# Attention on one core: sixteen softmax groups on VectorE with three passes each, in place of fourteen with three to four, and a new written-out order

## The chip, the cores and the metric

The kernel runs on one core of a Trainium2 chip. The metric is the device time of one execution in microseconds (us), here the median of three runs. The core's engines work side by side, each on its own instruction stream in order: TensorE (PE) multiplies matrices into PSUM, VectorE (DVE) and ScalarE (ACT) read PSUM and SBUF, GpSimd (POOL) works on SBUF here, and SyncE (SP) issues the DMAs.

## The reference

```python
# q, k, v: 8 batches x 8 heads x 512 positions x 64, float32
scale = 1.0 / np.sqrt(q.shape[-1])
scores = np.einsum('bhqd,bhkd->bhqk', q, k) * scale
attn = np.exp(scores - scores.max(axis=-1, keepdims=True))
attn = attn / attn.sum(axis=-1, keepdims=True)
out = np.einsum('bhqk,bhkd->bhqd', attn, v)
```

## The kernel before, in words

The 64 heads are taken as 32 pairs. For each pair, q and k are loaded in float32 (one 256 KB DMA each), cast to float16 by GpSimd, and turned so that the 64 features lie on partitions: 22 pairs, the first among them, by PE (steps `T`, followed by a VectorE copy `C` into the tile `tqk`), ten by a transposing DMA (steps `u`).

A **group** is 128 keys of both heads of a pair (for the first and last pair: two blocks of one head) against all 512 queries. Its scores fill one buffer `st` of 128x1024 float32 in PSUM (step `S`, L289: two matmuls that run side by side on the two halves of PE's rows). There are three such buffers; the number after the dot in `S57.0` is the buffer. The groups number 0 to 128; 127 and 128 are two halves of the last one. Most groups are exponentiated by ScalarE in one instruction (L295), which writes the float16 tile `pt`.

Fourteen groups (`KIND`) are exponentiated by VectorE instead, by building the float16's bits with a polynomial. For most of them PE first adds a constant to the scores (`lift`, L275, two more matmuls), so that the low 16 bits of a float32 score are the fraction of the exponent. Step `r` (L317) copies the scores from PSUM to a float32 tile `z`; steps `p` (L350, L331) are passes of `scalar_tensor_tensor` over 128x1024 elements. Kinds C and F take `r` and three passes, all on VectorE; S and X take `r` and two, with two GpSimd instructions (step `m`, L365 and L368) between them. The last pass of C, F and S reads `y` and `z`, both in SBUF, and writes 32-bit words to a tile `pd`. The buffer `st` of such a group is free again after the last pass that reads it.

Step `V` (L420) multiplies 128 queries of `pt` with v and a column of ones, four matmuls of 65 columns over the four blocks of keys; seven such results share one PSUM bank `o`. `R` and `N` (L385, L393) take the reciprocal of the ones' column and scale into the SBUF tile `ring`, and `O` stores 1 or 2 heads. `B` steps are matmuls on constants whose result is not used. `L` and `F` are V, R, N and the store for the last half head.

All of this is issued in the order of the string `ORDER`, written out by hand as one list of steps; each engine's instructions stand in the order in which the list names them, and waits between engines follow from the tiles. A cast step `cq4+p5.0` also waits for the VectorE step named behind the plus sign; 31 casts have such a wait. Pools set the rest: seven raw tiles for each of q, k and v (`RAW`), six of `qkp`, seven of `tqk`, 30 of `pt` and 4 of `pd`.

Of the kernel before, what the change touches and what calls it, by code (L numbers as in the profile page):

```python
# [37 lines left out]
T9.0.0 lk17 cq12 V4.0.3.39.1 T9.1.0 S34.2 cv6 lq16 V4.1.0.40.1 C9 V4.1.1.41.1 cq13 S35.0 lv13 R35.7
p30.1 T10.0.0 T10.1.0 lq17 S36.2 lk18 C10 S37.1 cv5+p30.1 S38.0 N35.7 ck12 T11.0.0 lv12 T11.1.0
p30.2 S39.2 V4.1.2.42.1 V4.1.3.43.1 V5.0.0.44.1 S40.1 C11 cv7+p30.1 ck13 r39 S41.0 lv14 T12.0.0 cv8  # L40
lq18 T12.1.0 S42.1 lk19 cv10 C12 V5.0.1.45.1 lq19 V5.0.2.46.1 ck14 V5.0.3.47.1 p39.0 V5.1.0.48.1
O21.1 S43.0 V5.1.1.49.0 O35.1 V5.1.2.50.0 V5.1.3.51.0 V6.0.0.52.0 lv15 S44.1 R42.7 ck15 p39.1
V6.0.1.53.0 lk20 ck16 S45.0 cq14+r39 lk21 V6.0.2.54.0 N42.7 S46.2 V6.0.3.55.0 p39.2 lv17 T13.0.1
T13.1.1 S47.1 lk22 R49.7 S48.0 C13 cv9+R49.7 O42.1 S49.2 r47 cv12 V6.1.0.56.1 V6.1.1.57.1
V6.1.2.58.1 cq15 V6.1.3.59.1 S50.0 N49.7 lv16 V7.0.0.60.1 ck17 V7.0.1.61.1 V7.0.2.62.1 p47.0 S51.2
lq20 V7.0.3.63.0 cv11 V7.1.0.64.0 V7.1.1.65.0 lq21 V7.1.2.66.0 S52.0 cq16 R56.7 N56.7 V7.1.3.67.0
lq22 V8.0.0.68.0 ck18+N49.7 p47.1 S53.2 lq23 V8.0.1.69.0 T14.0.1 cq17 T14.1.1 lk23 S54.0 R63.7 C14
S55.1 cq18+R63.7 lv19 N63.7 S56.2 T15.0.1 O49.1 p47.2 T15.1.1 V8.0.2.70.0 V8.0.3.71.0 lk24
V8.1.0.72.0 S57.0 C15 lq24 S58.1 V8.1.1.73.0 r57 V8.1.2.74.0 ck19+C15 T16.0.1 lk25 T16.1.1 S59.2
cq19 lv18 V8.1.3.75.0 C16 V9.0.0.76.0 cq20 S60.1 O56.1 R70.7 ck20 V9.0.1.77.1 N70.7 lq25 S61.2 p57.0  # L50
V9.0.2.78.1 V9.0.3.79.1 O63.1 T17.0.0 cq21+p47.2 T17.1.0 S62.1 cv13+C1 lk26 C17 S63.0 V9.1.0.80.1
V9.1.1.81.1 p57.1 lk27 V9.1.2.82.1 S64.2 V9.1.3.83.1 lq26 V10.0.0.84.0 V10.0.1.85.0 V10.0.2.86.0
R77.7 cv15+C17 V10.0.3.87.0 V10.1.0.88.0 N77.7 V10.1.1.89.0 lq27 V10.1.2.90.0 ck21+p57.0 S65.0 R84.7
S66.1 N84.7 T18.0.1 lk28 S67.2 p57.2 lv20 V10.1.3.91.0 T18.1.1 V11.0.0.92.0 lv22 S68.0 C18
ck22+p57.2 lq28 r68 S69.1 cq22+C18 T19.0.1 lk29 V11.0.1.93.0 cq23 V11.0.2.94.0 S70.2 O70.1 p68.0
ck23 V11.0.3.95.0 T19.1.1 V11.1.0.96.0 cq24 V11.1.1.97.0 S71.1 R91.7 S72.0 m68.0 N91.7 S73.2 u22 C19
S74.1 r72 T20.0.1 V11.1.2.98.0 T20.1.1 u23 V11.1.3.99.0 S75.2 C20 V12.0.0.100.0 V12.0.1.101.0 p72.0
S76.1 lk30 cv14 V12.0.2.102.0 V12.0.3.103.0 V12.1.0.104.0 V12.1.1.105.1 ck24 S77.2 lv21 R98.7 p72.1
V12.1.2.106.1 lq29 ck25 S78.1 u24 V12.1.3.107.1 N98.7 cq25 V13.0.0.108.1 V13.0.1.109.1 S79.0 p68.2
V13.0.2.110.1 T21.0.0 u25 T21.1.0 V13.0.3.111.1 S80.1 C21 ck26 S81.2 S82.0 cq26+r5 R105.7 lq30 r81  # L60
V13.1.0.112.0 V13.1.1.113.0 O77.1 V13.1.2.114.0 cq27 V13.1.3.115.0 V14.0.0.116.0 S83.1 lq31 cv16
V14.0.1.117.0 N105.7 V14.0.2.118.0 cq28 lv23 S84.0 p81.0 V14.0.3.119.1 cv17 lk31 V14.1.0.120.1
V14.1.1.121.1 V14.1.2.122.1 S85.1 cv19 R112.7 V14.1.3.123.1 N112.7 V15.0.0.124.1 ck27 V15.0.1.125.1
S86.0 lv24 R119.7 p81.1 V15.0.2.126.0 lv26 V15.0.3.127.0 V15.1.0.128.0 ck28 V15.1.1.129.0
V15.1.2.130.0 S87.1 cv18 N119.7 V15.1.3.131.0 V16.0.0.132.0 S88.2 cv21+R119.7 lv25 R126.7
V16.0.1.133.1 N126.7 V16.0.2.134.1 cq29 O91.1 V16.0.3.135.1 V16.1.0.136.1 V16.1.1.137.1 S89.0 u26
p72.2 V16.1.2.138.1 V16.1.3.139.1 V17.0.0.140.0 V17.0.1.141.0 S90.2 V17.0.2.142.0 R133.7 ck29 O98.1
V17.0.3.143.0 N133.7 V17.1.0.144.0 S91.1 u27 p81.2 V17.1.1.145.0 S92.0 S93.2 V17.1.2.146.0
V17.1.3.147.1 r93 V18.0.0.148.1 cv20+p81.2 lv28 V18.0.1.149.1 V18.0.2.150.1 S94.1 O105.1 cq30
V18.0.3.151.1 V18.1.0.152.1 R140.7 V18.1.1.153.1 ck30 u28 N140.7 S95.0 S96.2 cv22 R147.7  # L70
V18.1.2.154.0 N147.7 V18.1.3.155.0 cv23 V19.0.0.156.0 V19.0.1.157.0 O112.1 V19.0.2.158.0
V19.0.3.159.0 p93.0 lv27 S97.0 V19.1.0.160.0 V19.1.1.161.1 V19.1.2.162.1 V19.1.3.163.1 R154.7
cv25+C2 V20.0.0.164.1 S98.2 N154.7 S99.1 m93.0 u29 S100.0 r99 V20.0.1.165.1 V20.0.2.166.1
V20.0.3.167.1 V20.1.0.168.0 V20.1.1.169.0 lv29 S101.2 V20.1.2.170.0 R161.7 O119.1 V20.1.3.171.0
N161.7 V21.0.0.172.0 V21.0.1.173.0 S102.0 u30 p99.0 V21.0.2.174.0 V21.0.3.175.1 V21.1.0.176.1
V21.1.1.177.1 V21.1.2.178.1 cv24+r99 S103.2 R168.7 V21.1.3.179.1 O126.1 cv26+R161.7 N168.7
V22.0.0.180.1 V22.0.1.181.1 S104.1 O133.1 R175.7 m99.0 S105.0 N175.7 V22.0.2.182.0 O147.1
V22.0.3.183.0 V22.1.0.184.0 O154.1 V22.1.1.185.0 V22.1.2.186.0 p93.2 V22.1.3.187.0 S106.2 O161.1
V25.0.0.188.0 O161.0 S107.1 V25.0.1.189.1 R182.7 V25.0.2.190.1 lv30 N182.7 S108.0 V25.0.3.191.1 r108
V25.1.0.192.1 V25.1.1.193.1 V25.1.2.194.1 S109.2 V25.1.3.195.1 V23.0.0.196.0 V23.0.1.197.0 R189.7  # L80
V23.0.2.198.0 S110.0 N189.7 cq31 S111.1 p99.2 S112.2 V23.0.3.199.0 V23.1.0.200.0 V23.1.1.201.0
V23.1.2.202.0 V23.1.3.203.1 V26.0.0.204.1 ck31+r5 R196.7 S113.0 r111 V26.0.1.205.1 cv27+C2 u31
S114.2 cv28 V26.0.2.206.1 N196.7 V26.0.3.207.1 V24.0.0.208.1 V24.0.1.209.1 S115.0 O168.0 R203.7
V24.0.2.210.0 p108.0 V24.0.3.211.0 O175.1 V24.1.0.212.0 S116.2 O182.1 V24.1.1.213.0 V24.1.2.214.0
N203.7 lv31 V24.1.3.215.0 m108.0 S117.0 p111.0 O189.1 V26.1.0.216.0 V26.1.1.217.1 O203.1
# [15 lines left out]
def kernel(  # L101
# [29 lines left out]
    for m, kind in KIND.items():  # L131
        (g, c, _), (g2, c2, _) = groups[m]
        assert 0 < g == g2 < LAST and c == c2
        if kind in LIFTED:
            raises.setdefault(g, set()).add(c)
# [126 lines left out]
    def scores(m, b):  # L262
# [34 lines left out]
        )  # L297

# [331 lines left out]
```

## Time and profile before

| | before |
|---|---|
| three runs | 116.27, 116.42, 116.73 us; median 116.42 |
| the profiled execution | 116.05 us, of which span 114.3 us |
| ScalarE busy | 107.0 us, 94% of the span, 119 instructions |
| TensorE busy | 103.8 us, 91%, 1549 matmuls |
| VectorE busy | 103.5 us, 91%, 178 instructions |
| GpSimd busy | 76.5 us, 67%, 110 instructions |
| granted TensorE clock | full in each of the 40 slices |

The busy time of an engine is the time in which at least one of its instructions was under way. Instructions of one engine overlap at their ends, so the mean duration of one is longer than the distance from its start to the start of the next; where rates matter, distances between starts are the measure. The profiled execution lies 0.37 us below the median of the three runs.

### The profile page before, as it was taken

How to read it: one execution, taken by the hardware profiler on the slowest of the kernel's cores; microseconds unless marked ns; L12 is line 12 of the kernel's file. 1: busy time of each engine (PE TensorE's matmuls, PEld its weight loads, DVE VectorE, ACT ScalarE, POOL GpSimd, SP SyncE). 2: the span in 40 equal slices, each digit the busy share in tenths (PEclk: the TensorE clock that was granted, in tenths of full speed). 3: DMA queues.
4: the chain of work that ended last, by engine and by line, in shares of the span. 5: the costliest groups of instructions: out<-in, count | busy, mean ns of one | idle time of the engine just before them, and what ended most of it. 6: DMA issues, size and time to landing. Idle time of an engine off the chain costs nothing.

```text
span 114.3 us, 3938 instructions
## 1 busy us (share of the span) xinstructions
PE 103.8 (91%) x1549; PEld 65.7 (57%) x1549; DVE 103.5 (91%) x178; ACT 107.0 (94%) x119; POOL 76.5 (67%) x110
## 2 busy tenths in 40 slices
PE   7979899998899898999998899999999999999970
PEld 5635555565564564655665466675567666676660
DVE  4457999999999999999999999999999999999660
ACT  4499999999999999999999999999999999999960
POOL 2348755295968957927749999991799999384300
PEclk9999999999999999999999999999999999999999
DMA  2999999999999999999999998989959899999864
GB/s 92 276 317 373 384 380 382 383 385 373 384 388 367 363 382 382 372 384 388 373 376 383 373 215 260 172 267 384 272 147 312 238 327 151 383 333 366 290 231 146
DMA packets 45619, 36.44 MB, mean 319 GB/s; under 512 B 12704, under 2 KB 45600, under 8 KB 45600
## 3 DMA queue, kind: packets, MB, share of 16 engines
q1 hardware_dynamic: 45168, 35.86, 103.8%
q10 hardware_dynamic: 432, 0.33, 0.9%
q8 instruction: 12, 0.20, 0.6%
q14 instruction: 7, 0.06, 0.1%
HBM read 25.17 MB, written 8.39 MB: 294 GB/s over the span
## 4 chain that ended last, share of the span: by engine, by line
DVE 32%; PE 31%; ACT 26%; issue 5%; DMA 2%; ACTq 0%
ACT pt L295 24%; PE o L420 14%; PE st L289 13%; DVE y L350 12%; DVE tqk L254 5%; DVE ring L393 4%; DVE pd L350 4%; DVE z L317 4%; DMA q<-in_q_dram 2%; ACT pt L527 2%; DVE rc L385 1%; PE tp L234 1%; PE o L430 1%; DVE obl L461 1%; PE st L275 0%
## 5 line engine op out<-in xcount | busy, mean ns | idle before, releaser
L295 ACT ACTIVATE pt<-st 128x1024 f16<-128x1024 f32 (+1 forms) x112 | 102.1, 1113 | 0.4 <-PE st L289 0.4
L289 PE MATMUL st<-tqk 64*128 64x512 f16 (+1 forms) x250 | 47.0, 380 | 5.2 <-ACT pt L295 3.3
L420 PE MATMUL o<-vp,pt 128*128 128x65 f16 x912 | 45.4, 195 | 0.0
L420 PEld LDWEIGHTS <-pt 128*128 128x128 f16 x912 | 36.2, 98 | 14.4 <-issue 13.3
L195 POOL CAST vp<-v 128x512 f16<-128x512 f32 x32 | 24.1, 768 | 10.4 <-DVE pd L350 4.2
L289 PEld LDWEIGHTS <-tqk 64*128 64x128 f16 x250 | 14.4, 93 | 17.9 <-issue 8.2
L393 DVE TENSOR_TENSOR ring<-o,rc 128x448 f32<-128x448 f32 (+2 forms) x37 | 22.5, 608 | 1.0 <-DVE rc L385 0.2
L209 POOL CAST qkp<-q 128x512 f16<-128x512 f32 x30 | 18.1, 612 | 2.9 <-DVE rc L385 1.4
L317 DVE TENSOR_SCALAR z<-st 128x1024 f32<-128x1024 f32 x14 | 17.0, 1213 | 1.3 <-PE st L289 1.1
L209 POOL CAST qkp<-k 128x512 f16<-128x512 f32 x19 | 13.6, 719 | 5.7 <-issue 2.4
L350 DVE SCALAR_TENSOR_TENSOR pd<-y,z 128x1024 uint32<-128x1024 f32 x12 | 15.3, 1272 | 0.0
L420 PE MATMUL o<-vp,pd 128*128 128x65 f16 x96 | 15.1, 195 | 0.1
L350 DVE SCALAR_TENSOR_TENSOR y<-st,z 128x1024 f32<-128x1024 uint16 x12 | 14.5, 1212 | 0.0
L234 PE MATMUL tp<-ident,qkp 128*128 128x128 f16 x168 | 14.0, 220 | 0.4 <-POOL qkp L206 0.4
L254 DVE COPY tqk<-tp 128x1024 f16<-128x1024 f16 x20 | 13.6, 681 | 0.1
L234 PEld LDWEIGHTS <-qkp 128*128 128x128 f16 x168 | 9.7, 97 | 4.0 <-issue 1.7
L420 PEld LDWEIGHTS <-pd 128*128 128x128 f16 x96 | 9.4, 98 | 2.8 <-issue 2.2
L350 DVE SCALAR_TENSOR_TENSOR y<-st,y 128x1024 f32<-128x1024 uint16 x9 | 10.9, 1208 | 0.0
L206 POOL TENSOR_SCALAR qkp<-k 128x512 f16<-128x512 f32 x12 | 7.4, 617 | 5.0 <-DVE pd L350 3.5
L385 DVE RECIPROCAL rc<-o 128x7 f32<-128x7 f32 (+2 forms) x37 | 7.2, 196 | 1.5 <-PE o L420 1.3
L365 POOL TENSOR_SCALAR t<-y 128x1024 f32<-128x1024 f32 x4 | 4.2, 1044 | 2.4 <-DVE y L350 2.1
L368 POOL TENSOR_TENSOR y<-t,y 128x1024 f32<-128x1024 f32 x2 | 5.6, 2780 | 0.2
(57 smaller groups left out, 46.7 us busy)
## 6 DMA issues: line engine op xcount, KB each, us to landing
v<-in_v_dram SPq DMA_DIRECT2D x32, 256.0 KB, 5.4
k<-in_k_dram SPq DMA_DIRECT2D x31, 256.0 KB, 5.5
q<-in_q_dram SPq DMA_DIRECT2D x31, 256.0 KB, 5.4
out_dram<-ring SPq DMA_DIRECT2D x29, 256.0 KB, 4.5
out_dram<-ring SPq DMA_DIRECT2D x5, 128.0 KB, 3.5
k<-in_k_dram ACTq DMA_DIRECT2D x2, 128.0 KB, 2.7
q<-in_q_dram SPq DMA_DIRECT2D x2, 128.0 KB, 2.9
tqk<-qkp SPq DMA_TRANSPOSE x10, 5.3
```

The lines of the kernel that those rows point to most:

```text
L195: return nc.gpsimd.tensor_copy(out=vps[g % NV][:, :, :, 0:D], in_=raw[g]["v"][:, :, :, :])
L206: return nc.gpsimd.tensor_scalar(out=dst, in0=src[:, :, :, :], scalar1=128.0 * LOG2E, scalar2=1.0, op0=AluOp.mult, op1=AluOp.mult)
L209: return nc.gpsimd.tensor_copy(out=dst, in_=src[:, :, :, :])
L234: nc.tensor.transpose(tps[g][:, n, i, :], qkp[g][:, n, i, :], ident)
L254: nc.vector.tensor_copy(out=tqk[g][:, :, :], in_=tps.pop(g).rearrange("p n i c -> p n (i c)"))
L289: nc.tensor.matmul(st[:, x, cols], kc, qc[:, cols], start=kind is None or kind not in LIFTED, stop=True)
L295: nc.scalar.activation(out=pt[:, :, cols], in_=st[:, :, cols], func=EXP, scale=by)
L317: nc.vector.tensor_scalar(out=r["z"][:, :, :], in0=r["st"][:, :, :], scalar1=2.0**17 if lifted else 1.0 if groups[m][0][0] in raises else ...
L350: nc.vector.scalar_tensor_tensor(out=r["bits"][:, :, :] if last else y, in0=(zero, one, y)[s], scalar=(QUARTIC if quartic else CUBIC)[s], ...
L385: dve(nc.vector.reciprocal(out=rcs[u][:, 0:n], in_=o[:, x : x + n, D : D + 1]))
L393: nc.vector.tensor_tensor(out=ring[:, u % NU : u % NU + n, :], in0=o[:, x : x + n, 0:D], in1=rc[:, 0:n].broadcast_to([P, n, D]), op=AluOp. ...
L420: nc.tensor.matmul(os[u // 7][:, u % 7, :], blocks[(g, c, h)][:, y * P : (y + 1) * P], vps[g % NV][:, h, c, :], start=(c == 0), stop=(c == ...
```

## The change

Sixteen groups instead of fourteen go to VectorE, one of them (group 3) in the first pair, and some next to each other in one pair (45, 46, 47 and 88, 89). All sixteen are lifted by PE. Each takes three steps on VectorE, all of which read `st` in PSUM: `r` and `p0` build the product `t` of two linear factors, GpSimd squares `t` (`m`, one instruction), and `p2` adds the square to the scores and writes 16-bit words to `pt`. No `z` and no `pd` is left. A step's last number says whether it covers half 0, half 1, or both (2): of the `r`, 7 cover both halves and 18 one; the 32 `p0` and the 32 `p2` cover one each; of the squares, one covers both and 30 one. `st` is held until the last `p2`. Nine pairs are turned by DMA instead of ten. No cast waits for a named VectorE step any more. The `pt` pool has 40 tiles.

The core of the diff:

```diff
-RAW, QK16, TQK, NV = 7, 6, 7, 12
-KIND = {5: "C", 12: "C", 20: "C", 30: "C", 39: "C", 47: "C", 57: "F", 68: "S", 72: "C", 81: "C", 93: "X", 99: "S", 108: "X", 111: "C"}
-BY_DMA = (22, 23, 24, 25, 26, 27, 28, 29, 30, 31)
+RAW, QK16, TQK, NV, NP16 = 7, 6, 7, 12, 40
+BY_VECTOR = (3, 10, 23, 30, 45, 46, 47, 50, 55, 85, 88, 89, 93, 104, 108, 114)
+BY_DMA = (20, 21, 22, 24, 26, 27, 28, 29, 30)
...
-ck1 cq1 S3.2 T1.0.0 T1.1.0 ck2 C1 cq2 S4.1 S5.0 cv0 S6.2 r5 T2.0.1 T2.1.1 cq3 S7.1 ck3 V0.0.0.4.0 C2
+ck1 S3.2 cq1 T1.0.0 B12.1.1 B12.1.1 r3.1 cq2 T1.1.1 B12.1.1 C1 ck2 p3.0.1 S7.1 S5.0 r3.0 T2.0.0 cv0
...
-        if kind in ("X", "Q"):
+        if by_vector:
             bits = ppool.tile([P, 2, S], U16, tag="pt", name=f"pt_{m}")
             pt = bits.bitcast(FP16)
-        elif kind:
-            bits = dpool.tile([P, 2, S], U32, tag="pd", name=f"pd_{m}")
-            pt = bits.bitcast(FP16).rearrange("p x (s n) -> p x s n", n=2)[:, :, :, 0]
-            for x, (_, _, h) in enumerate(grp):
-                s = slice(64 * h, 64 * h + 64)
+            for x in range(2):
+                s = slice(64 * x, 64 * x + 64)
                 nc.tensor.matmul(st[:, x, :], lift[s], ones[s, 0:S], start=True, stop=False)
...
+    def raise_(m, h):
+        r, h = raised[m], part(h)
...
+                out=r["t"][:, h],
+                in0=fraction(r["st"])[:, h],
+                scalar1=ROOTS[0],
+                scalar2=Q2**0.5,
+                op0=AluOp.add,
+                op1=AluOp.mult,
...
+    def pass_(m, s, h):
+        r, h = raised[m], part(h)
+        t = r["t"][:, h]
+        if s == 0:
...
+                    out=t,
+                    in0=fraction(r["st"])[:, h],
+                    scalar=ROOTS[1],
+                    in1=t,
...
+                out=r["bits"][:, h],
+                in0=r["st"][:, h],
+                scalar=BOTTOM,
+                in1=r["y"][:, h],
...
+    def square(m, h, engine):
...
+        return engine.tensor_tensor(out=r["y"][:, h], in0=t, in1=t, op=AluOp.mult)
+
+    def middle(m, h):
+        square(m, h, nc.gpsimd)
```

What the new order does is seen at three places. The first is VectorE at the start of the kernel. `tqk_1` is the second pair's turned q and k, without which none of its groups can start. Before, its two copies stand next to each other, and the first lifted group is 5:

```order
L203 CAST qkp_1_239<-q32_1_110 128x2x2x64
L248 COPY tqk_1_248<-tp_1_0_249 128x512
L248 COPY tqk_1_248<-tp_1_1_255 128x512
L317 TENSOR_SCALAR z_5_281<-st_5_269 128x1024
L254 COPY tqk_2_283<-tp_2_0_284 128x1024
```

After, on the same engine at the same place, group 3 is the first:

```order
L203 CAST qkp_1_236<-q32_1_107 128x2x2x64
L253 COPY tqk_1_246<-tp_1_0_247 128x512
L325 TENSOR_SCALAR t_3_256<-st_3_238 128x512
L253 COPY tqk_1_246<-tp_1_1_260 128x512
L340 SCALAR_TENSOR_TENSOR t_3_256<-st_3_238,t_3_256 128x512
```

The first half of group 3's `r` has moved between the two copies, and ScalarE, which had group 3 at this point, goes from group 2 to group 7 of the second pair.

The second place is one lifted group in the middle, on VectorE. Before, group 30 (with `tqk_9`, `tqk_10` and two banks of results between its steps):

```order
L317 TENSOR_SCALAR z_30_741<-st_30_720 128x1024
L393 TENSOR_TENSOR ring_85<-o_4_654,rc_28_739 128x448
L350 SCALAR_TENSOR_TENSOR y_30_778<-st_30_720,z_30_741 128x1024
L254 COPY tqk_9_780<-tp_9_0_781 128x1024
L385 RECIPROCAL rc_35_824<-o_5_743 128x7
L350 SCALAR_TENSOR_TENSOR y_30_778<-st_30_720,y_30_778 128x1024
L254 COPY tqk_10_827<-tp_10_0_828 128x1024
L393 TENSOR_TENSOR ring_85<-o_5_743,rc_35_824 128x448
L350 SCALAR_TENSOR_TENSOR pd_30_721<-y_30_778,z_30_741 128x1024
```

After, group 85; x2 stands for two halves in a row, and the square `y_85` comes from GpSimd:

```order
L325 TENSOR_SCALAR t_85_1923<-st_85_1907 128x1024
L259 COPY tqk_25_1893<-tp_25_0_1894 128x1024
L340 SCALAR_TENSOR_TENSOR t_85_1923<-st_85_1907,t_85_1923 128x512 x2
L377 RECIPROCAL rc_140_2004<-o_20_1925 128x7
L385 TENSOR_TENSOR ring_82<-o_20_1925,rc_140_2004 128x448
L351 SCALAR_TENSOR_TENSOR pt_85_1908<-st_85_1907,y_85_1993 128x512 x2
```

Four passes have become three, and the last one, which read two SBUF tiles, now reads `st` and one SBUF tile.

The third place is ScalarE at the end. Before, the last five instructions:

```order
L295 ACTIVATE pt_124_2603<-st_124_2602 128x1024
L295 ACTIVATE pt_125_2610<-st_125_2609 128x1024
L295 ACTIVATE pt_126_2657<-st_126_2656 128x1024
L295 ACTIVATE pt_127_2666<-st_127_2665 128x2x256
L295 ACTIVATE pt_127_2666<-st_128_2720 128x2x256
```

After:

```order
L301 ACTIVATE pt_121_2637<-st_121_2636 128x1024
L301 ACTIVATE pt_126_2673<-st_126_2672 128x1024
L301 ACTIVATE pt_122_2687<-st_122_2686 128x1024
L301 ACTIVATE pt_125_2693<-st_125_2692 128x1024
L301 ACTIVATE pt_127_2380<-st_128_2785 128x2x256
```

Group 127 has moved ahead of this piece. On PE, 18 steps of V and L (72 matmuls of 65 columns) stand between the scores of 125 and those of 128; before, 11 such steps stand between 127 and 128.

More of the change, by code (lines that the diff above doesn't have):

```diff
@@ L129 @@
     groups += [tail, tail]
-    raises = {}
[L131 to L135, printed above, removed]
+    scaled = set()
+    for m in BY_VECTOR:
+        (g, c, h), (g2, c2, h2) = groups[m]
+        assert m == 3 or 0 < g == g2 < LAST and c == c2
+        scaled |= {(g, h), (g2, h2)}
+    to_bits = 128.0 * LOG2E
     cpool = ctx.enter_context(tc.tile_pool(name="const", bufs=1))
@@ L278, in scores @@
         else:
-            pt = last["pt"] = ppool.tile([P, 2, S], FP16, tag="pt", name=f"pt_{m}")
+            pt = ppool.tile([P, 2, S], FP16, tag="pt", name=f"pt_{m}")
+        if half == 0:
+            last["pt"] = pt
         for x, (g, c, h) in enumerate(grp):
@@ L316, in raise_ @@
+    def raise_(m, h):
+        r, h = raised[m], part(h)
+        if "t" not in r:
+            r["t"] = wpool.tile([P, 2, S], FP32, tag="z", name=f"t_{m}")
         dve(
             nc.vector.tensor_scalar(
-                out=r["z"][:, :, :],
-                in0=r["st"][:, :, :],
-                scalar1=2.0**17 if lifted else 1.0 if groups[m][0][0] in raises else 128.0 * LOG2E,
-                scalar2=None if lifted else 143.0 * 1024,
-                op0=AluOp.max if lifted else AluOp.mult,
@@ L416, in values @@
             heads.append((g, h, u))
[L417 to L418 removed]
+        o = unit_bank(u, bank)
         for c in range(NI):
             nc.tensor.matmul(
[L421 removed]
+                o[:, u % 7, :],
                 blocks[(g, c, h)][:, y * P : (y + 1) * P],
@@ L426, in values, with unit_bank, fill @@
             )
-    def fill(u, n):
+    def unit_bank(u, bank):
+        if u // 7 not in os:
+            os[u // 7] = ps_x.tile([P, 7, D + 1], FP32, tag=f"x{bank}", name=f"o_{u // 7}")
+        return os[u // 7]
+    def fill(u, n, bank):
         x = u % 7
         nc.tensor.matmul(
-            os[u // 7][:, x : x + n, :].rearrange("p x d -> p (x d)"),
+            unit_bank(u, bank)[:, x : x + n, :].rearrange("p x d -> p (x d)"),
             ones[:, 0:P],
```

246 lines of the change are left out of this document (112 added, 134 removed).

## The prediction

> **What bounds the kernel now.** I read the page first, then ScalarE's timeline.
>
> ```profile
> PE 103.8 (91%) x1549; PEld 65.7 (57%) x1549; DVE 103.5 (91%) x178; ACT 107.0 (94%) x119; POOL 76.5 (67%) x110
> ```
>
> Three engines are busy for over 90%, so shares alone name no bound. The timeline of ScalarE does (start, length, instruction, count; merged while it has no gap):
>
> ```profile
> 8.22 12.95 ACT L295 ACTIVATE pt<-st 128x1024 f16<-128x1024 f32 x14
> 19.96 6.71 ACT L295 ACTIVATE pt<-st 128x1024 f16<-128x1024 f32 x7
> 8.22 101.52 ACT L295 ACTIVATE pt<-st 128x1024 f16<-128x1024 f32 x111
> 110.11 0.60 ACT L295 ACTIVATE pt<-st 128x512 f16<-128x512 f32 x1 [0.37 <-PE st L289]
> ```
>
> The first and second row come from overlapping stretches: the fourteenth exp starts at 19.96, so thirteen take (19.96 - 8.22) / 13 = 0.903 us each, start to start. From group 3 at 8.22 ScalarE never lies idle by the view until the last half group. Yet 110 whole exps at 0.903 and a half one of some 0.65
>
> ```profile
> L295 ACT ACTIVATE pt<-st 128x512 f16<-128x512 f32 x2 | 1.3, 650 | 0.4 <-PE st L289 0.4
> ```
>
> make 100.0, and the 111-exp row says 101.52: 1.5 us are lost in starts that come late without a visible gap. ScalarE sets the pace, and PE, which refills the buffers in order with its other work, sets these late starts. GpSimd and VectorE collide besides:
>
> ```profile
> 28.00 1.22 DVE L350 SCALAR_TENSOR_TENSOR pd<-y,z 128x1024 uint32<-128x1024 f32 x1
> 28.04 1.65 POOL L209 CAST qkp<-k 128x512 f16<-128x512 f32 x1
> 77.03 1.61 DVE L350 SCALAR_TENSOR_TENSOR pd<-y,z 128x1024 uint32<-128x1024 f32 x1
> 18.11 0.62 POOL L195 CAST vp<-v 128x512 f16<-128x512 f32 x1
> ```
>
> Against `pd<-y,z`, whose inputs both lie in SBUF, a cast takes 1.65 instead of 0.62, or the pass 1.61 instead of 1.22.
>
> **The change part by part.** The sum is made on the profiled execution: 116.05 us, span 114.3 and 1.75 outside it. It lies 0.37 below the median of 116.42, which is added back at the end.
>
> *ScalarE's work.* Of the row of 110 whole exps, 108 remain, since 16 groups go to VectorE for 14: 2 x 0.903 = **-1.81**.
>
> *The start.* Group 3 no longer fills ScalarE's time from 8.22; its next is group 7, which needs both copies of `tqk_1`.
>
> ```profile
> 6.78 0.38 PE L289 MATMUL st<-qt,kt 64*128 64x512 f16 x2
> 7.09 0.62 PE L234 MATMUL tp<-ident,qkp 128*128 128x128 f16 x8
> 7.53 0.75 DVE L248 COPY tqk<-tp 128x512 f16<-128x512 f16 x2 [0.66 <-PE tp L234]
> 8.34 0.39 PE L289 MATMUL st<-tqk 64*128 64x512 f16 x2 [0.63 <-ACT pt L527]
> 8.57 0.38 PE L275 MATMUL st<-const-bfloat16-1.0,lift 64*128 64x512 bf16 x2
> 8.78 0.38 PE L289 MATMUL st<-tqk 64*128 64x512 f16 x2
> ```
>
> Group 3's scores now begin with two lift matmuls (8.57 to 8.78: 0.21), so the transposes of k move from 7.09 to 7.3 and the first copy from 7.53 to about 7.74. Half an `r` (0.60, below) follows at about 8.08 and ends at 8.68; q's transposes wait for the first copy, because they now use the same bank, and are ready about then. The second copy takes 0.42 to 9.10, PE's scores 0.45 with the signals, and the exp starts at 9.6 instead of 8.22: **+1.37**. So moving group 3 saves nothing by itself; the gain of this and the step above together is 0.44.
>
> *VectorE.* The price of a pass goes by distances between starts:
>
> ```profile
> 31.05 0.61 DVE L393 TENSOR_TENSOR ring<-o,rc 128x448 f32<-128x448 f32 x1
> 31.58 1.21 DVE L350 SCALAR_TENSOR_TENSOR y<-st,z 128x1024 f32<-128x1024 uint16 x1
> 32.71 0.68 DVE L254 COPY tqk<-tp 128x1024 f16<-128x1024 f16 x1
> 33.30 0.19 DVE L385 RECIPROCAL rc<-o 128x7 f32<-128x7 f32 x1
> 33.42 1.17 DVE L350 SCALAR_TENSOR_TENSOR y<-st,y 128x1024 f32<-128x1024 uint16 x1
> ```
>
> 1024 elements take 1.13 and 448 take 0.53; on the line between them 512 take 0.60, so a split costs about 0.06. No row has a 512-element float32 pass; the bounds are half of 1.13 and the ring row's 0.53 plus the full difference, 0.57 to 0.65. Before there are 52 passes, 58.8 us; after, 7 whole and 82 halves, 57.1, and one more copy of 0.59. VectorE's work falls by some 1.1 less 0.6, against 1.8 for ScalarE: VectorE is a little closer to the pace than it was. The Trainium skill ("VectorE: DVE Perf Modes", the section "The TRN2 errata — SBUF-src ops pay a fixed extra latency per instruction") has a rule that speaks against halves: an instruction that reads PSUM costs 120 cycles beside its elements at 0.96 GHz, by estimate 0.125 us for each split, so that the 41 splits would cost 5.1 us instead of 2.5 and the sum would rise by up to 2.6. By that rule 448 elements take 0.59 where the ring row has 0.53; the trace is against it.
>
> *GpSimd.* The first three rows are the old middle steps by group; the third of them is a square of one tile, the form that all sixteen take now, and the last two rows give its distance to the next instruction:
>
> ```profile
> L365 POOL TENSOR_SCALAR t<-y 128x1024 f32<-128x1024 f32 x4 | 4.2, 1044 | 2.4 <-DVE y L350 2.1
> L368 POOL TENSOR_TENSOR y<-t,y 128x1024 f32<-128x1024 f32 x2 | 5.6, 2780 | 0.2
> L368 POOL TENSOR_TENSOR y<-t 128x1024 f32<-128x1024 f32 x2 | 3.8, 1892 | 0.2
> 100.11 1.89 POOL L368 TENSOR_TENSOR y<-t 128x1024 f32<-128x1024 f32 x1
> 101.94 0.61 POOL L195 CAST vp<-v 128x512 f16<-128x512 f32 x1
> ```
>
> From start to start 1.83 a group, 16 x 1.83 = 29 us, for 4.2 + 5.6 + 3.8 = 13.6: GpSimd rises from 76.5 to about 92 busy, and falls by what the collisions cost, since no pass has two SBUF inputs now. I take it as hidden: its casts lead their users, and it stays below ScalarE's 98.7 (108 whole and two half exps). If its queue runs late, the square is late, and with it `p2`; that is a rival below.
>
> *PE.* Per ScalarE group PE has two matmuls of scores, eight of V, and some transposes:
>
> ```profile
> 25.14 0.39 PE L289 MATMUL st<-tqk 64*128 64x512 f16 x2
> 25.46 0.56 PE L420 MATMUL o<-vp,pt 128*128 128x65 f16 x12
> 25.95 0.39 PE L289 MATMUL st<-tqk 64*128 64x512 f16 x2
> 108.17 1.58 PE L420 MATMUL o<-vp,pt 128*128 128x65 f16 x44
> 109.69 0.39 PE L289 MATMUL st<-tqk 64*128 64x256 f16 x2
> ```
>
> Scores to V takes 0.32, a V matmul 0.033, and the step from V back to scores 0.13. With eight transposes at 0.5 and lifts at 0.21, the order before sums to 91.5 us of PE from group 3 to the end, the new one to 94.0: four more lifts, one more pair turned, 9 more returns from V to scores. The spread matters more. Taken between the fills of successive ScalarE groups, PE's work before has stretches of 1.89, 1.82, 1.69 and 1.61; after, the longest ahead of the tail is 1.33 and all others are at most 1.2. From group 46 on ScalarE has two buffers, the third being held by VectorE. An exp lasts 1.11 from start to end,
>
> ```profile
> L295 ACT ACTIVATE pt<-st 128x1024 f16<-128x1024 f32 (+1 forms) x112 | 102.1, 1113 | 0.4 <-PE st L289 0.4
> ```
>
> after which its buffer can be filled in some 0.43 with signals; with 1.81 between two exps on one buffer a fill may come up to 0.3 late without cost. Stretches of up to 1.2 fit. Of the 1.5 lost, 1.37 fall before group 121; I take 0.55 for what is left of them: **-0.8**. The bounds are 0 (all fit) and 1.4 (as now), or 4 by the second rival.
>
> *The tail.* The first row is groups 120 to 127:
>
> ```profile
> 102.67 7.07 ACT L295 ACTIVATE pt<-st 128x1024 f16<-128x1024 f32 x8
> 110.76 0.30 PE L446 MATMUL o_last<-vp,pt 128*128 128x65 f16 x4 [0.21 <-ACT pt L295]
> 111.30 0.29 DVE L461 TENSOR_TENSOR obl<-o_last,rc_last 128x128 f32<-128x128 f32 x1
> 111.62 0.35 ACTq L468 DMA_DIRECT2D out_dram<-obl x1
> ```
>
> From group 121's exp at 103.6 it is 10.7 us to the end of the span, with six whole exps and two halves. After, it is four and a half; PE has 18 steps of V and L, 2.76 us by the prices above, between the scores of 125 and of 128, and ScalarE waits for it by 0.8. The rest is the chain of the other three rows. 128's scores start 4.13 after 121's exp; from there (109.69 before) to the end it took 4.6 and will take some 4.8, with two more VectorE steps ahead of the last. 8.93 against 10.7 less the 2.3 of the exps that have moved ahead: **+0.54**.
>
> *Sum:* 116.05 - 1.81 + 1.37 - 0.8 + 0.54 = 115.35, and with 0.37 for the median **115.7**, 0.6% below 116.42.
>
> *DMA.* One transposing DMA less, and no PE wait on one in the waits of before: nothing.
>
> **Rivals.** First, *PE sets the pace in the second half*. By the prices, from group 70's scores to the end PE has 43.2 us and ScalarE 42.7; at group 119 the gap is 1.8, of which 0.9 is the usual lead. If PE keeps the idle it has ahead of score matmuls,
>
> ```profile
> L289 PE MATMUL st<-tqk 64*128 64x512 f16 (+1 forms) x250 | 47.0, 380 | 5.2 <-ACT pt L295 3.3
> ```
>
> 5.2 us over the kernel, 2.2 over this part, its last matmul starts at 110.5 instead of 110.9, the longer tail takes 0.15 back and late starts ahead of group 70 0.3: on the median 116.5, no change. For it: PE gained work while ScalarE lost some. Against: much of that idle is waiting for ScalarE, which would go.
>
> Second, *the chain of a lifted group is longer than its slot* (slower). One buffer serves the lifted groups from 46 on: the scores of the next can start only after the last `p2`. In six of the fifteen slots there are six exps, 5.42 us. VectorE's steps from `r` to the last `p2`, with the copies and R, N between, sum to 4.8 there; scores with lift take 0.65 and signals 0.15: 5.6, already over, by less than the 0.3 that a fill may be late. Each half also waits for its square, half of 1.83, and for what is queued ahead of that on GpSimd. If that adds 0.4 in the six short slots and 0.1 in nine others, 3.3 us come on and the 0.55 go: 118.4. It decides as soon as the scores of a lifted group start over 5.7 after those of the one before in such a slot. Against: VectorE works on the other half meanwhile, and the slots of seven exps have 0.2 to 0.9 to spare.
>
> Third, *the halves or squares don't cost what they should*: that price is within the second.
>
> **How the numbers follow.** The forecast, with late starts between 0 and 0.7 (115.1 to 115.8): 0.48. PE as the pace, or late starts as before, about 116.5: 0.27. The chain, 117 to 119: 0.25. A measurement can tell some 0.5% from no change, 0.58 us: faster is below 115.84, slower above 117.0. The range leaves out the chain's worse half: 114.9 to 117.8.
>
> **What would show it.** In the profile after: the second pair's first exp at about 9.6; thirteen exps in 11.74 without late starts; no GpSimd cast over 0.7 and no pass over its own length; halves at 0.60 start to start; 0.8 of ScalarE idle ahead of the last exp. The forecast is wrong if ScalarE shows gaps before lifted groups' scores (the chain), if PE has no idle at all in the second half (PE), or if the exp of group 7 starts far from 9.6.

## The result, and the profile after

The changed kernel takes 119.83 us (median of four runs, 118.70 to 121.43) against 116.49: 1.026 times the time before, 95% interval 1.022 to 1.030. It is slower; forecast were 115.7 us and 114.9 to 117.8. Executions disturbed at a lower clock are left out of the ratios here, not of the medians (of the changed kernel the slowest, without which its median is 119.53, of the one with fewer stores the two slowest).

The page of the changed kernel, with the rows that answer to those of before (profiled execution: 119.53 us, span 117.4, so 2.13 outside it):

```profile
PE 105.4 (90%) x1565; PEld 67.0 (57%) x1565; DVE 103.1 (88%) x216; ACT 106.5 (91%) x117; POOL 88.4 (75%) x133
L301 ACT ACTIVATE pt<-st 128x1024 f16<-128x1024 f32 (+1 forms) x110 | 101.5, 1062 | 3.2 <-PE st L296 3.0
L366 POOL TENSOR_TENSOR y<-t 128x512 f32<-128x512 f32 (+1 forms) x31 | 32.8, 1069 | 7.8 <-DVE rc L377 4.3
L214 POOL CAST qkp<-q 128x512 f16<-128x512 f32 x30 | 18.2, 615 | 2.3 <-DMA q<-in_q_dram 0.9
```

ScalarE has as little to do as forecast, but 3.0 us of visible waits for scores where it had 0.4. Its timeline (start, length, line, count, idle time before and what ended it) shows where:

```profile
9.81 82.54 ACT L301 ACTIVATE pt<-st 128x1024 f16<-128x1024 f32 x89 [1.65 <-PE st L296]
92.52 15.70 ACT L301 ACTIVATE pt<-st 128x1024 f16<-128x1024 f32 x17 [0.17 <-PE st L296]
108.40 2.85 ACT L301 ACTIVATE pt<-st 128x1024 f16<-128x1024 f32 x3 [0.18 <-PE st L296]
112.23 0.60 ACT L301 ACTIVATE pt<-st 128x512 f16<-128x512 f32 x1 [0.98 <-PE st L296]
```

Group 121's exp, the last of the seventeen in the second row, starts at 107.20; by the forecast it would have been 104.67 (113.6 of span less 8.93). The miss of 4.18 us in the profiled execution divides into: group 7 at 9.81 instead of 9.6, 0.2; from group 7 to group 121, 2.3; from 121's exp to the end of the span 10.2 instead of 8.93, 1.3; outside the span, 0.4.

For the 2.3 in the middle, the waits of the changed kernel (engine, line, what it waited for, sum, times, longest) show a releaser that PE did not have before, the transposing DMA:

```profile
POOL y L366 <- DVE rc L377: 4.3, 5, 2.0
POOL y L366 <- DVE t L340: 3.1, 6, 1.0
PEld L239 <- POOL qkp L214: 2.0, 5, 0.9
PEld L296 <- DMA tqk<-qkp: 1.2, 2, 0.6
PE st L296 <- DMA tqk<-qkp: 1.0, 2, 0.5
SPq L189 <- POOL qkp L214: 8.9, 12, 2.0
```

The last row is SyncE's queue: loads wait there for a raw tile until GpSimd has cast what is in it. Before, the same wait was a third of that:

```profile
SPq L189 <- POOL qkp L209: 2.9, 7, 0.8
```

Two pieces of the chain that ended last put these rows in order (start, length, what; dots stand for steps left out):

```profile
66.69 5.27 DMA tqk<-qkp
...
72.01 0.39 PE st L296 x2
...
74.67 0.21 DVE rc L377
...
74.90 2.04 POOL y L366 x2
76.94 0.61 POOL vp L195
...
77.65 7.24 DMA tqk<-qkp
...
85.01 0.62 POOL qkp L214
85.63 0.56 POOL vp L195
86.19 0.56 POOL qkp L214
...
88.65 1.05 POOL y L366
...
89.72 0.70 DVE pt L351
...
90.47 0.39 PE st L280 x2
```

First a turn, for whose tile PE waits until 72.0 us. Then two half squares, a cast, a turn that lands 7.24 us later, then casts, a square, and the last pass of a lifted group, for which PE's lift waits. ScalarE is not in these pieces. Was the cause GpSimd, the DMA engines, PE, or the chain of the lifted group? The windows from 10 to 66 us and from 66 to 105 us (busy time by engine; PE clock, share of the DMA engines and GB/s at the end), before:

```profile
10.00:66.00 56.00, 51.55 (x718) 31.31 (x716) 55.51 (x78) 56.00 (x63) 39.14 (x60) 1.00 1.09 378
66.00:105.00 39.00, 38.41 (x673) 25.55 (x670) 38.22 (x60) 39.00 (x44) 31.30 (x38) 1.00 1.15 272
```

and after:

```profile
10.00:66.00 56.00, 52.09 (x725) 32.24 (x726) 53.27 (x97) 56.00 (x62) 51.64 (x76) 1.00 1.05 348
66.00:105.00 39.00, 37.44 (x619) 24.25 (x615) 36.66 (x70) 38.63 (x43) 29.98 (x43) 1.00 1.13 287
```

GpSimd, the fifth number, goes from 39.14 to 51.64 of 56 us, 92%, while the mean over its whole span is 75%. It casts for later pairs in that time, so its work lies early; the average hid that. The DMA engines move less there (348 instead of 378 GB/s).

### The profile page after: what moved, and what is told of

The parts are those of the page before. It is cut to its first block, busy times and chain, and to the rows that moved or that the text cites. A ratio compares the mean times of both kernels' runs of the same rounds, so it can differ in the third digit from the quotient of the medians.

```text
span 117.4 us, 3977 instructions
## 1 busy us (share of the span) xinstructions
PE 105.4 (90%) x1565; PEld 67.0 (57%) x1565; DVE 103.1 (88%) x216; ACT 106.5 (91%) x117; POOL 88.4 (75%) x133
## 4 chain that ended last, share of the span: by engine, by line
ACT 27%; DMA 21%; PE 20%; POOL 16%; DVE 7%; issue 4%; SPq 1%; POOLq 0%
ACT pt L301 27%; DMA tqk<-qkp 11%; PE o L411 11%; PE st L296 8%; POOL y L366 7%; DMA k<-in_k_dram 7%; POOL qkp L214 5%; DMA out_dram<-ring 4%; POOL vp L195 3%; DVE t L325 2%; DVE pt L351 2%; POOL qkp L206 1%; PE st L280 1%; DVE ring L385 1%; SPq L471 1%
## 5 line engine op out<-in xcount | busy, mean ns | idle before, releaser
L411 PE MATMUL o<-vp,pt 128*128 128x65 f16 x1008 | 49.1, 195 | 0.7 <-DVE tqk L259 0.4
L411 PEld LDWEIGHTS <-pt 128*128 128x128 f16 x1008 | 38.3, 98 | 19.3 <-issue 17.0
L366 POOL TENSOR_TENSOR y<-t 128x512 f32<-128x512 f32 (+1 forms) x31 | 32.8, 1069 | 7.8 <-DVE rc L377 4.3
L351 DVE SCALAR_TENSOR_TENSOR pt<-st,y 128x512 uint16<-128x512 f32 x32 | 21.4, 682 | 1.1 <-POOL y L366 1.0
L340 DVE SCALAR_TENSOR_TENSOR t<-st,t 128x512 f32<-128x512 uint16 x32 | 21.6, 680 | 0.3
L195 POOL CAST vp<-v 128x512 f16<-128x512 f32 x32 | 19.3, 617 | 2.9 <-DMA v<-in_v_dram 2.6
L325 DVE TENSOR_SCALAR t<-st 128x512 f32<-128x512 uint16 (+1 forms) x25 | 20.5, 835 | 0.8 <-PE st L296 0.7
L280 PE MATMUL st<-const-bfloat16-1.0,lift 64*128 64x512 bf16 x32 | 6.3, 378 | 0.3 <-DVE pt L351 0.2
L426 PE MATMUL o<-const-bfloat16-1.0 128*128 128x65 bf16 x44 | 4.9, 196 | 0.0
L475 PE MATMUL st_0a<-const-bfloat16-1.0 128*128 128x256 bf16 (+1 forms) x17 | 3.5, 387 | 0.8 <-PEq L619 0.8
L426 PEld LDWEIGHTS <-const-bfloat16-1.0 128*128 128x128 bf16 x44 | 2.8, 98 | 1.6 <-issue 1.6
```

Source lines behind the costliest of these rows:

```text
L195: return nc.gpsimd.tensor_copy(out=vps[g % NV][:, :, :, 0:D], in_=raw[g]["v"][:, :, :, :])
L325: nc.vector.tensor_scalar(out=r["t"][:, h], in0=fraction(r["st"])[:, h], scalar1=ROOTS[0], scalar2=Q2**0.5, op0=AluOp.add, op1=AluOp.mult,)
L340: nc.vector.scalar_tensor_tensor(out=t, in0=fraction(r["st"])[:, h], scalar=ROOTS[1], in1=t, op0=AluOp.add, op1=AluOp.mult,)
L351: nc.vector.scalar_tensor_tensor(out=r["bits"][:, h], in0=r["st"][:, h], scalar=BOTTOM, in1=r["y"][:, h], op0=AluOp.add, op1=AluOp.add,)
L366: return engine.tensor_tensor(out=r["y"][:, h], in0=t, in1=t, op=AluOp.mult)
L411: nc.tensor.matmul(o[:, u % 7, :], blocks[(g, c, h)][:, y * P : (y + 1) * P], vps[g % NV][:, h, c, :], start=(c == 0), stop=(c == NI - 1),)
```

## The experiments

All ratios are to the kernel before, run on the same chip. Theory A is GpSimd's queue; the rivals are D (the DMA engines set the pace), PE (it sets the pace from some point on), and the chain of the lifted group.

**Without squares.**

```diff
     def middle(m, h):
-        square(m, h, nc.gpsimd)
+        raised[m]["y"] = raised[m]["t"]
```

> The changed kernel without the squares on GpSimd: the last pass of each lifted group reads t where it read y, so the result of the sixteen groups is left out of the computation as far as the square goes. Theory A (GpSimd's queue): the squares, 32.8 us, hold up casts behind them, the casts hold up loads and turns, and the PE waits for tiles; without them GpSimd falls to about 56 us busy, the DMA engines stay full between 28 and 65 us, PE's waits for turned tiles (2.2 us) go, and the time falls to 116 to 117.5. Rival D (the DMA engines are full from 10 to 105 us and set the pace whatever GpSimd does): 119 to 120. Rival PE (PE's work sets the pace in the second half): 119 or more.

Measured: 117.71 us (117.56 to 118.72), ratio 1.014 (1.008 to 1.021). The windows of this kernel:

```profile
10.00:66.00 56.00, 52.19 (x727) 32.52 (x725) 53.44 (x97) 56.00 (x62) 35.08 (x61) 1.00 1.07 358
66.00:105.00 39.00, 38.52 (x639) 25.33 (x637) 37.24 (x73) 38.95 (x43) 16.88 (x29) 1.00 1.15 288
```

Squares cost 2.1 us by the two medians and 1.4 us by the two ratios (1.026 and 1.014). Group 121's exp comes at 106.03 and no wait on a transposing DMA is left: the turn that PE waited for at 72.0 us is issued at 65.22 instead of 66.69 us, with group 7's exp at 9.78 and 9.81. GpSimd now waits 19.3 us for loads of `v` (2.6 in the changed kernel), and SyncE's waits for casts of `qkp` fall from 8.9 to 4.5. The DMA engines move no less than in the changed kernel (358 and 288 GB/s, there 348 and 287), so they alone do not set the pace. But this takes both the work off the queue and the square out of the chain.

**Squares read by nobody.** The squares stay; the last pass reads `t`.

```diff
-                in1=r["y"][:, h],
+                in1=r["t"][:, h],
```

> The changed kernel with its squares still issued on GpSimd at the same places, but read by nobody: the last pass of each lifted group reads t, so the square is left out of the result. GpSimd's queue has the same work and the same waits as in the changed kernel; only VectorE no longer waits for the squares. Queue theory (squares in GpSimd's queue hold up casts, late casts hold up loads and turns): as the changed kernel, 119 to 121. Chain theory (what hurts is that the last pass comes a square later, so the buffer of the lifted groups comes free late): as without squares, 117 to 118.

Measured: 119.67 us (119.16 to 120.30), ratio 1.025 (1.019 to 1.032). All of the loss is back though nobody waits for a square: the queue, not the chain. VectorE's half passes have the same mean length here and without squares (0.680 us for the middle one), so the squares do not act by slowing VectorE's instructions.

**Fewer stores.**

```diff
         del heads[: 1 + both]
+        if both and 2 <= g < 14:
+            return
```

> The changed kernel without the stores of pairs 2 to 13: twelve transfers of 256 KB, about 8 us of all 16 DMA engines, are left out. Theory D (the DMA engines set the pace from 65 us on): turned tiles land in 4 us instead of 5 to 7, PE's waits for them go, 116 to 117.5. Theory A (GpSimd's queue): GpSimd's casts wait less for their loads, but the squares still hold up casts: 118.5 to 119.5. Rival PE: 119.5.

Measured: 118.20, 118.78, 121.05 and 121.88 us; ratio 1.019 (1.014 to 1.024). In the profiled execution (118.20) group 121 comes at 105.52 and the waits for turned tiles are gone too, with GpSimd as busy as in the changed kernel (51.51 of 56 us). So there the same work on GpSimd made no late tile: a full DMA queue is part of the cause. The ratio lies between those of the changed kernel (1.026) and of the one without squares (1.014); the two lower times lie above what theory D expects, around the lower end of theory A's range. Alone this tells little.

**Two pairs turned by PE**, which also takes work off the DMA engines:

```diff
-u21
 T23.0.0 cq26 S66.0
...
 C23
+T21.0.0 T21.1.0 C21
...
 C25
+T26.0.0 T26.1.0 C26
 V17.1.0.144.1
-u26
```

> The changed kernel with pairs 21 and 26 turned by PE and a copy on VectorE instead of by DMA, right behind the copies of pairs 23 and 25: the two pairs whose turned tiles PE waited for (2.2 us together). The DMA engines lose two turns of about 2.1 us each, PE gains 1.0 us, VectorE 1.2 us. Theory that late turns behind a full DMA queue cost the time: the waits for pairs 21 and 26 go, 118 to 118.7, if other tiles (loads, the other turns) come earlier too 117.5. Rival (VectorE's two copies lie in the chain of groups 88 and 85 and cost 0.6 each): 120 or more.

Measured: 121.74 us (121.66 to 122.53), ratio 1.044 (1.038 to 1.050). Two turns less by DMA, no wait of PE on a turned tile left, and 1.9 us slower than the changed kernel. Less work for the DMA engines gained nothing here, but the edit also adds VectorE's work, so it does not decide on theory D. In its waits GpSimd's squares wait longer for VectorE than before (13.6 instead of 7.4 us):

```profile
POOL y L366 <- DVE t L340: 7.9, 7, 2.6
POOL y L366 <- DVE rc L377: 5.7, 5, 2.2
```

VectorE's two copies fit; that they are the cause was not tried by itself.

**Less PE**, with the squares as they are:

```diff
-        for c in range(NI):
+        n = NI if g < 10 else 3
+        for c in range(n):
```

> The changed kernel with three of the four matmuls of each V step from pair 10 on: 176 matmuls of 0.033 us, 5.8 us of PE, are left out (the last quarter of the keys does not enter the outputs of these pairs). Rival PE (PE sets the pace in the second half): PE catches up, the late starts of ScalarE after group 50 go, 116 to 117. Theories A and D (tiles come late, PE waits for them): PE waits longer for the same tiles; only its catching up is quicker, 118 to 119.

Measured: 120.44 us (119.93 to 121.06), ratio 1.036 (1.031 to 1.041). 5.8 us of matmuls less, and no faster: PE does not set the pace in the second half. In the profiled execution (120.68) the granted clock is at half from 74.1 to 77.5 us; the two quickest executions, 119.93 and 120.20, gain nothing either.

**Halves joined.** Steps on one half are dropped at the first and done on both at the second.

```diff
-m46.1
...
-m46.0
+m46.2
 N42.7
...
-p46.2.1
...
-p46.2.0
+p46.2.2
 T15.0.0
```

> The changed kernel with its halves joined: each pass, r and square of a lifted group is done once over both halves, at the place of the second half. VectorE has 41 instructions less (2.5 us at 0.06 each), GpSimd 15 less; the chain of a lifted group loses the overlap of one half's square with the other half's pass, about 1 us each. Rival B (the chain is longer than its slot): the six short slots lengthen by 1 us each, 122 to 126. Theory A: squares of 1.89 in one piece hold up casts longer at once, 120 to 121. If neither counts, the shorter VectorE work shows: 119.

Measured: 137.18 us (136.87 to 139.24), ratio 1.179 (1.175 to 1.183). 17.4 us, 1.1 for each of the sixteen groups, not only in the six short slots. Its waits:

```profile
ACT pt L297 <- PE st L292: 16.4, 22, 1.7
DVE pt L347 <- POOL y L362: 16.1, 14, 1.5
PE st L276 <- DVE pt L347: 13.8, 13, 1.9
```

Read from the bottom: PE's lift waits for the last pass, that for the square, and ScalarE for PE. This is the second rival as the prediction drew it. In the changed kernel the same wait of the last pass is 1.0 us in all: the halves keep the chain inside its slot, barely.

**How much, or when?** If GpSimd's queue it is, is it the amount of work, or squares at its head that wait for VectorE with casts behind them? Four kernels ask. Half squares, read by nobody as above:

```diff
-        return engine.tensor_tensor(out=r["y"][:, h], in0=t, in1=t, op=AluOp.mult)
+        y, n = r["y"][:, h], slice(0, S // 2)
+        return engine.tensor_tensor(out=y[:, n], in0=t[:, n], in1=t[:, n], op=AluOp.mult)
```

> As the kernel with the squares aside (nobody reads them, the last pass reads t), but each square does only half the columns: the 31 instructions stay at their places in GpSimd's queue with the same waits on VectorE, and take about 0.55 instead of 1.04 us, 15 us less in all, some 7 of them between 10 and 66 us, where GpSimd was busy for 92% of the time. Load theory (GpSimd has too much work up to 66 us): most of the gap to the kernel without squares goes, 117.8 to 118.7. Wait theory (the squares' waits on VectorE at the head of the queue hold up the casts, 7 us in all): as the changed kernel, 119.3 to 120.3.

Measured: 118.93 us (118.51 to 119.03), ratio 1.020 (1.011 to 1.030); GpSimd 44.73 of 56 us from 10 to 66 us. Short casts of v:

```diff
-                out=vps[g % NV][:, :, :, 0:D], in_=raw[g]["v"][:, :, :, :]
+                out=vps[g % NV][:, :, :, 0 : D if g < 4 else 4],
+                in_=raw[g]["v"][:, :, :, 0 : D if g < 4 else 4],
```

> The changed kernel with all its squares, but the casts of v write only 4 of 64 columns from pair 4 on, and V reads the v of pairs 0 to 3 instead (so the outputs of the other pairs are left out): 28 casts some 0.5 us shorter, 14 us of GpSimd less, 7 of them before 66 us, at other places of the queue than the squares. Load theory: as with half squares, 117.8 to 118.7. Wait theory, or any theory by which the squares themselves are what hurts: 119.3 to 120.3.

Measured: 119.33 us (118.35 to 119.98), ratio 1.024 (1.014 to 1.035); GpSimd 46.37 of 56. The first lies between the theories. The second lies just inside the range of the wait theory, and so against the load theory. Squares read by nobody and three casts later in the queue:

```diff
-m50.1
...
-m50.0
...
 cv16
+m50.1 m50.0
```

> As the kernel with the squares aside (full squares, 33 us of GpSimd, read by nobody; the last pass reads t), but each square stands three casts later in GpSimd's queue, so that VectorE has long written its input and no cast stands behind a waiting square. GpSimd has the same work as in the changed kernel and none of the 7 us of waits on VectorE at the head of its queue. Wait theory: the time falls to that without squares, 117.5 to 118.3. Load theory (33 us of squares are too much work up to 66 us, waits or not): 119.2 to 120.2. If both count alike: 118.4 to 119.1.

Measured: 120.62 us (119.47 to 121.67), ratio 1.035 (1.030 to 1.040). No wait of a square on VectorE is left among its waits, PE's score matmuls no longer wait for a turned tile (1.0 us in the changed kernel), and yet the time does not fall. Other waits have come in (the last row is the window from 46 to 66 us):

```profile
POOL qkp L214 <- DMA q<-in_q_dram: 2.6, 2, 2.4
PE tp L239 <- POOL qkp L214: 1.8, 1, 1.8
46.00:66.00 20.00, 17.46 (x217) 10.06 (x214) 16.32 (x31) 16.87 (x20) 17.35 (x27) 0.83 0.96 320
```

GpSimd waits 2.4 us for a load of `q`, PE's transposes 1.8 us for a cast soon after, and then the granted clock is at half from 52.8 to 59.6 us. Three of ScalarE's starts come late there, by 3.5 us together. This profile is of the slowest of the six executions (121.67). The quickest, 119.47, is as slow as the kernel with the squares at their places (119.16 to 120.30). So what the wait theory expected, 117.5 to 118.3, came in none of the six; but as the edit made other tiles late, it does not refute the theory. Sixteen casts moved ahead of the square before them, in the whole kernel:

```diff
+ck20
 m50.0 V10.1.1.89.1 V10.1.2.90.1 p50.2.1 V10.1.3.91.0 S69.1
-ck20
```

> The changed kernel, whole, with sixteen casts moved one or two places up in GpSimd's queue, ahead of the square that stood before them. It is the remedy that the wait theory asks for: a cast runs while a square would still wait for VectorE. Price: a square that would not have waited comes 0.6 later, and with it the last pass of its half. Wait theory: 118.2 to 119.2. Load theory: 119.5 to 120.5. If the chains of the lifted groups decide (the rival of the prediction; joined halves cost 17 us): 121 or more.

Measured: 121.64 us (121.32 to 121.77), ratio 1.045 (1.042 to 1.048). 1.8 us slower: the chain's price. Its last passes wait 4.8 us for squares instead of 1.0, and PE's lifts 3.2 us for the passes:

```profile
DVE pt L351 <- POOL y L366: 4.8, 10, 1.5
PE st L280 <- DVE pt L351: 3.2, 5, 1.5
```

Is it the amount, then? By GpSimd's busy time from 10 to 66 us: 51.5 (aside) 119.67; 46.4 (short casts) 119.33; 44.7 (half squares) 118.93; 35.1 (none) 117.71. PE's score matmuls wait 1.1, 0.8, 0.4 and 0 us for turned tiles in these four profiles. The order is that of the load, but the first three times cannot be told apart with certainty, and the kernel with squares later (48.9 us, 120.62) does not fit into it. So it is shown that squares in GpSimd's queue cost the time; how much of that is their amount and how much their waiting at the head is not.

**The start and the tail.** Group 3 given back to ScalarE, its steps taken out of the order, with squares and without:

```diff
-BY_VECTOR = (3, 10, 23, 30, 45, 46, 47, 50, 55, 85, 88, 89, 93, 104, 108, 114)
+BY_VECTOR = (10, 23, 30, 45, 46, 47, 50, 55, 85, 88, 89, 93, 104, 108, 114)
```

> The changed kernel with group 3 given back to ScalarE: fifteen lifted groups, the steps r3, p3 and m3 gone, all else in the same order. The step of the prediction on the start said that lifting group 3 saves nothing by itself (one exp of 0.90 against 1.37 at the start). By that, group 3's exp starts at about 8.2 and group 7's at about 9.2 instead of 9.8, and the time falls by 0.5 to 0.7, to 119.1 to 119.4 where the rest stays. Rival: GpSimd and VectorE, with 2 and 4 us less to do before 16 us, cast pairs 3 to 6 earlier, loads follow earlier, and the late tiles go too: 117.5 to 118.5. If the start was not held by group 3: 119.8 to 120.7.

Measured: 119.77 us (118.79 to 122.69), ratio 1.023 (1.015 to 1.031). In its trace group 3's exp starts at 7.93 and group 7's at 9.66: one exp more, and still 0.15 earlier than in the changed kernel. That says little: in the other profiled executions with group 3 lifted, group 7's exp starts anywhere from 9.19 to 10.15. By the median nothing is left of it.

> The kernel without squares (last pass reads t) and, besides, group 3 given back to ScalarE. Without late tiles the start shows by itself: the prediction priced lifting group 3 at 1.37 against 0.90 saved. By that the whole schedule behind comes 0.5 earlier, and with the start measured in the changed kernel (group 7 at 9.8) 0.7: 117.0 to 117.3. If the start hangs on something else than group 3 (the first pair's chain): 117.7 plus up to 0.9.

Measured: 117.67 us (116.93 to 119.08, ten runs), ratio 1.009 (1.006 to 1.013), against 117.71 with group 3 lifted. Two pairs of medians differ by 0.06 and 0.04: in the new order lifting group 3 neither costs nor gains, and the 0.5 to 0.7 expected from undoing it did not come. Without the filling matmuls of units 220 and 228:

```diff
-B228.1.1 B228.1.1 B228.1.1
...
-B228.1.1 B220.1.0
```

> The changed kernel without the 20 filling matmuls of units 220 and 228 that PE runs between 102 and 107 us (their results are overwritten). PE theory for the tail (from 90 us on PE has no idle, and the last half exp waits 1.1 us for PE's V steps): 20 x 0.033 = 0.66 us less of PE, the exp of 128 starts 0.5 to 0.7 earlier, 119.1 to 119.4. If ScalarE's exps set the tail: no change, 119.8. If the fills keep TensorE's clock up: a clock below 1.0 after 102 us, and slower than 120.

Measured: 120.18 us (119.06 to 120.31), ratio 1.026 (1.018 to 1.034): no gain; from 121's exp to that of 128 it takes 5.00 instead of 5.03 us. The granted clock is full up to PE's last matmul at 113.4 us without the fills too. All of these fills stand ahead of 121's scores, so the tail itself was not tested by this. Without squares and with three of four matmuls in V from pair 3 on:

```diff
-        for c in range(NI):
+        n = NI if g < 3 else 3
+        for c in range(n):
```

> The kernel without squares and, besides, three of four matmuls in each V step from pair 3 on: 232 matmuls, 7.6 us of PE, are left out, spread over the kernel. It asks where the late starts come from that stay without late tiles (1.6 us from group 7 to group 121, forecast 0.55) and the longer tail. If they are PE's stretches between two fills: late starts fall below 0.6, the last exp comes 0.5 closer to that of 121, 115.6 to 116.4. If they are set by ScalarE or by the order of buffers: 117.2 to 117.7.

Measured: 117.02 us (116.45 to 119.10, ten runs), ratio 1.005 (1.001 to 1.009). From 121's exp to 128's it takes 4.62 instead of 5.03 (4.54 in the first kernel with less PE), so PE's work does set that stretch; but the late starts from group 7 to 121 sum to 1.4 (1.6 without squares). So V's stretches on PE are not what mainly sets them. None of the kernels beats the one before.

## Why the prediction was wrong

One term was put at nothing that costs 1.4 to 2.1 us: GpSimd's squares. Two terms of the sum were mis-sized besides, the late starts and the tail, and of each about 1.0 us stays when the squares go. The terms one by one:

- *ScalarE's work*, -1.81: right in its count; 108 whole exps and two halves remain.
- *The start*, +1.37: right within 0.2, which is less than this start moves from execution to execution. "Moving group 3 saves nothing by itself" was right as well, though its price by the two terms was a loss of 0.47 and the runs without squares show 0.0.
- *VectorE*: right. Half passes that follow each other start 0.60 apart in the median, as the second and third of these rows do:

```profile
103.93 0.69 DVE L325 TENSOR_SCALAR t<-st 128x512 f32<-128x512 uint16 x1
104.66 0.69 DVE L340 SCALAR_TENSOR_TENSOR t<-st,t 128x512 f32<-128x512 uint16 x1
105.27 0.68 DVE L325 TENSOR_SCALAR t<-st 128x512 f32<-128x512 uint16 x1
105.86 0.20 DVE L377 RECIPROCAL rc<-o 128x7 f32<-128x7 f32 x1
```

  By the rule of the Trainium skill that the prediction weighed ("VectorE: DVE Perf Modes", "The TRN2 errata — SBUF-src ops pay a fixed extra latency per instruction") a half pass would by estimate take 0.66; these rows have 0.61 and 0.59.

- *GpSimd*, "taken as hidden": the step that failed. The argument set 92 us of work against ScalarE's 98.7 over the whole kernel, but 51.6 us of the work fall between 10 and 66 us. A half square is also 0.98 us from start to start, not half of 1.83. Price by the runs: 1.4 to 2.1 us. The rival named it ("what is queued ahead of that on GpSimd"), but as a delay of the square in its chain; the runs show delayed casts, loads and turns.
- *DMA*, "nothing": wrong in kind. One turn less was counted; that turns would be issued later, because their casts are late (one at 66.69 us, against 65.22 without squares), was not.
- *Collisions* vanish: right. All casts of 512 elements take 0.61 to 0.62, where some took 1.65.
- *Late starts*, -0.8: wrong, also without squares. By the same measure (distances between starts over 0.9035) it is 1.4 before, 1.6 without squares, 2.7 after, forecast 0.55. "Stretches of up to 1.2 fit" rested on PE's V work as the cause, and taking 7.6 us of that away left 1.4. Without squares the value is no better than "as now", the prediction's own upper bound of 1.4. What sets them stays open.
- *The tail*, +0.54: mis-sized by 1.3. The timeline at the end, PE's rows, then one of VectorE and one of SyncE:

```profile
108.66 0.82 PE L296 MATMUL st<-tqk 64*128 64x512 f16 x4
109.41 0.56 PE L411 MATMUL o<-vp,pt 128*128 128x65 f16 x12
109.80 0.41 PE L442 MATMUL o_last<-vp,pt 128*128 128x65 f16 x8
110.05 1.83 PE L411 MATMUL o<-vp,pt 128*128 128x65 f16 x52
111.81 0.39 PE L296 MATMUL st<-tqk 64*128 64x256 f16 x2
112.13 0.68 PE L411 MATMUL o<-vp,pt 128*128 128x65 f16 x16
113.07 0.42 DVE L385 TENSOR_TENSOR ring<-o,rc 128x256 f32<-128x256 f32 x1
113.66 0.45 SPq L403 DMA_DIRECT2D out_dram<-ring  x1
```

  128's scores start 4.6 after 121's exp, not 4.13, with PE never idle. From there to the end it takes 5.6, not 4.8: sixteen V matmuls (0.68) now stand behind 128's scores, and the last `ring` row and its store, which ends some 3.7 later, wait for them. Before, these V steps stood ahead of 128's scores and the same `ring` row started 0.58 after them (the row below, the scores at 109.69); now 1.26. The forecast followed the other store.

```profile
110.27 0.42 DVE L393 TENSOR_TENSOR ring<-o,rc 128x256 f32<-128x256 f32 x1
```

- *The rivals.* The second had the time (118.4) and the wrong mechanism here; joined halves and casts ahead show that it lies right behind. The first fell: less PE gave no time with squares, and without them 0.7 us, 0.4 of it between the exps of 121 and 128. The third did not apply.

The profiled execution without squares took 117.81, which is 2.46 above the sum of 115.35: 0.2 at the start, 1.2 from group 7 to group 121, 1.0 from there to the end of the span, 0.1 outside it. So of the miss of 4.18 us 1.7 go with the squares, and the larger part does not. Even without squares the kernel is slower than the one before (1.014).

## What to carry to other kernels

An engine "at 75%" may be full for half of the kernel: compare its work with the pace window by window, above all where it works ahead for others. In a queue that serves casts for loads and turns, added work can be paid by whoever stands behind the loads, several engines away; here two other orders of that queue did not buy it back. In a tail, follow each store back to its last matmul; a step put behind another moves the store that hangs on it.

## What the runs showed of the hardware

- A GpSimd square of one half, 128x512 in float32, takes 1.04 us, of both halves 1.89. From start to start it is 0.98 for a half (median of 22) and 1.83 for both, so halves cost 0.14 more a group, some 2 us of GpSimd over fifteen groups.
- The granted TensorE clock can drop to half within one execution: from 52.8 to 59.6 us in the profile with squares later, from 74.1 to 77.5 in the first with less PE. Why is not shown.
- A transposing DMA issued at 77.65 landed 7.24 us later (the chain above); the median from issue to landing is 5.3 in both kernels:

```profile
tqk<-qkp SPq DMA_TRANSPOSE x9, 5.3
```
